# Layer 1 of a hybrid encoder: which engine combines probability chunks, and how the sub-norm's sums of squares are multiplied

## The chip, the cores and the metric

The kernel runs on one core of a Trainium2 chip. The metric is the device time of one execution in microseconds (us). The engines of a core run their own instruction queues in order and wait for each other by semaphores: PE is TensorE (matmuls; PEld is its weight load), DVE is VectorE, ACT is ScalarE, POOL is GpSimd, SP issues most DMAs.

## What is computed

A two-layer encoder trunk over 2048 tokens of width 1024, in float32. Layer 0 (a sliding-window attention and a chunked attention, side by side) is not touched here. Layer 1 is a differential attention with 8 heads; cut to what matters:

```python
s1 = einsum(q1, k1) * scale          # 8 heads, q and k of width 64
s2 = einsum(q2, k2) * scale
p1 = softmax(where(mask, s1, -1e30))
p2 = softmax(where(mask, s2, -1e30))
a = p1 - lam * p2
o = einsum(a, v)                     # v of width 128 per head
...
o = rms_norm(o, subln_g) * (1.0 - lambda_init)   # per head, over the 128 values
y = (o.reshape(b, s, C_W) * silu(gate)) @ w_out
return x + y
```

The mask lets a block of 64 queries see all earlier blocks of 64 keys and its own.

## The kernel before

The kernel runs layer 0, then layer 1's input projection, then layer 1's mixer, `_mix1`. All that is told here lies in `_mix1`.

Tokens are cut into `NB` = 4 blocks (b) of 512, each with 4 rows of 128 queries (j). The work goes head by head and block by block, 32 pairs (h, b), here called heads for short: first the pairs with b = 0 and 1 in turn for each h (16 of them), then the 8 with b = 2, then the 8 with b = 3. For a pair, `scores` computes for each row and for both maps m (the two softmaxes) the scores of its keys in chunks of up to 512. For one chunk, PE makes two matmuls into a PSUM bank named cS (L913, L914, with queries split in a high and a low part), DVE finds the negative maximum cnm of each row (L917), and ACT writes the exponential into a probability tile named cP (L920). The bank of cS is free once ACT has read it; there are 4 of them.

After both maps of a row are done, DVE works out the reciprocals of the sums (crl, L931, L932), and each pair of chunks (one of each map) is joined to one: p1 is scaled by its reciprocal on POOL (L936), and then p2 is scaled and added. That second step has two forms. Ordinarily POOL scales p2 (L945) and adds it (L946). For every `COMB`-th pair, counted over the whole layer in `count`, DVE does both in one instruction (L943), for which it first multiplies two small factors (L942, tile cc) where a row has more than one chunk:

```python
nc.gpsimd.tensor_scalar(p1, p1, rl[:, 0:1], e1, ALU.mult, ALU.mult)
count[0] += 1
if count[0] % self.COMB == 0:
    ...
    nc.vector.scalar_tensor_tensor(p1, p2, c2, p1, ALU.mult, ALU.add)
else:
    nc.gpsimd.tensor_scalar(p2, p2, rl[:, 1:2], e2, ALU.mult, ALU.mult)
    nc.gpsimd.tensor_tensor(p1, p1, p2, ALU.add)
```

There are 320 such pairs of chunks in the layer.

`values` then transposes the joined chunks on PE (ctr, L959), copies each transposed tile out of PSUM into a tile cpt on ACT or, every third time, on DVE (L962, L964), and multiplies it with v into the output cO (L966, in float32, which stands as two records for each matmul in the trace). At the end of a head, `gate` copies cO out on ACT (cot, L981), squares it (csq, L983), makes part of the gate's sigmoid (L985, L986) and multiplies by the gate on POOL (L987). The rest of the head's sub-norm, `rest`, is put off to the third key tile of the next head's `values` (for the last head it follows at once): one float32 matmul with a tile of ones sums the squares over the 128 values (cms, L991, again two records), ACT takes the logarithm (L992), DVE adds (L993), ACT takes the exponential (L994), DVE multiplies (L995), and the result is split into high and low parts for the output projection.

Beside this main stream runs a side stream of PE work paced by a table (`STAGES1`): first the gate's projection (cG), then the output projection (com), both as three matmuls of rounded products (float32 rounded to the multiplier's format, dtype fp32r) at L214 to L216 per term. Values trail the scores by `LAG1` units. The order on each engine's queue is set when the program is built, by a scheduler that estimates each instruction's length and puts next what it takes to be ready; so a change of one instruction can shift the order of others nearby.

The pools: p1's chunks live in the pool `pp` with 20 buffers, p2's in 8 buffers of `sb`, the copied transposes in 6 buffers (tag "pt") of `sb`. A chunk's buffer of `pp` is held from its exponential to the last transpose that reads it.

Of the kernel before, what the change touches and what calls it, by code (L numbers as in the profile page):

```python
# [10 lines left out]
F32 = mybir.dt.float32  # L11
F32R = mybir.dt.float32r
AF = mybir.ActivationFunctionType
ALU = mybir.AluOpType
# [4 lines left out]
P = 128  # L19
# [4 lines left out]
BLK = NTB * P  # L24
# [7 lines left out]
def f32(ap):  # L32
    return ap.bitcast(F32)
# [52 lines left out]
class Trunk:  # L86
# [1 line left out]
    AHEAD = 2  # L88
    BANKS0, LAG0, SHARE0 = (3, 3, 1, 1), 9, 0.85
    FIN = 18  # L90
    COMB = 5
    BANKS1, LAG1 = (4, 2, 1, 1), (30, 30, 36, 36)
    STAGES1 = ((0, 0), (44, 84), (1088, 504))

# [762 lines left out]
    def _mix1(self, es):  # L857
        nc, tc, a, s = self.nc, self.tc, self.a, self.s1
        n = "c"
        pool = lambda nm, bufs, **kw: es.enter_context(tc.tile_pool(name=n + nm, bufs=bufs, **kw))  # L860
# [2 lines left out]
        ld = pool("ld", 2)  # L863
        yp = pool("y", 2 * KT)
        vp = pool("v", 4)
        pp = pool("pp", 20)
        kp = pool("kp", 4)
        sb = pool("sb", 2)
        NS, NTR, NO, NM = self.BANKS1
# [4 lines left out]
        mm = nc.tensor.matmul  # L874
# [17 lines left out]
        def scores(h, b, q, K, res, then):  # L892
# [4 lines left out]
            for j in range(NTB):  # L897
# [35 lines left out]
                for z, (c, ce) in enumerate(cuts):  # L933
# [3 lines left out]
                    count[0] += 1  # L937
                    if count[0] % self.COMB == 0:
                        c2 = rl[:, 1:2]
# [9 lines left out]
        def values(h, b, res):  # L949
            us = res["u"]  # L950
            O = pO.tile([P, BLK], F32, tag="O", name=n + "O")
            nkt = (b + 1) * NTB
            for kt in range(nkt):
                j0 = max(0, kt - b * NTB)
                wd = (NTB - j0) * P
                tp = ptr.tile([P, 512], F32, tag="tr", name=n + "tr")
                kk = (kt % 4) * P
                for j in range(j0, NTB):
                    nc.tensor.transpose(tp[:, (j - j0) * P:(j - j0 + 1) * P], us[j][kt // 4][:, kk:kk + P], self.ident)  # L959
                T = sb.tile([P, 512], F32, tag="pt", name=n + "pt", bufs=6)  # L960
                if kt % 3:
                    nc.scalar.activation(T[:, :wd], tp[:, :wd], AF.Copy)  # L962
                else:
                    nc.vector.tensor_copy(T[:, :wd], tp[:, :wd])  # L964
                v = res["v"][kt // 4][:, kk:kk + P]
                mm(O[:, j0 * P:], v, T[:, :wd], start=(kt == 0), stop=(kt == nkt - 1), skip_group_check=True)  # L966
                if kt == 2:
                    while normal:
                        normal.pop(0)()
                yield wd / P  # L970
            gate(h, b, O)
# [3 lines left out]
        def gate(h, b, O):  # L975

            rows, tok = slice(h * P, (h + 1) * P), slice(b * BLK, (b + 1) * BLK)
            g = sb.tile([P, BLK], F32, tag="g", name=n + "gg")
            nc.sync.dma_start(g, s["g"][rows, tok])
            o = ot.tile([P, BLK], F32, tag="ot", name=n + "ot")  # L980
            nc.scalar.activation(o, O, AF.Copy)  # L981
            sq = sb.tile([P, BLK], F32, tag="sq", name=n + "sq", bufs=1)
            nc.scalar.activation(sq, o, AF.Square)  # L983
            sg = sb.tile([P, BLK], F32, tag="sg", name=n + "sg", bufs=1)
            nc.scalar.activation(sg, g, AF.Exp, scale=-1.0)  # L985
            nc.scalar.activation(sg, sg, AF.Ln, bias=self.one)  # L986
            nc.gpsimd.tensor_tensor(o, o, g, ALU.mult)  # L987

            def rest():
                ms = ptr.tile([P, BLK], F32, tag="tr", name=n + "ms")  # L990
                mm(ms, f32(self.ones), sq, start=True, stop=True)  # L991
                nc.scalar.activation(sq, ms, AF.Ln, bias=self.eps, scale=1.0 / P)  # L992
                nc.vector.scalar_tensor_tensor(sg, sq, 0.5, sg, ALU.mult, ALU.add)  # L993
                nc.scalar.activation(sg, sg, AF.Exp, scale=-1.0)  # L994
                nc.vector.scalar_tensor_tensor(o, o, self.sub, sg, ALU.mult, ALU.mult)  # L995
                if b == 0 or (h, b) in place:
                    split(h, b, o)
                else:
                    nc.sync.dma_start(s["o"][rows, tok], o)
                ended.add((h, b))  # L1000

            normal.append(rest)
# [7 lines left out]
        def split(h, b, o):  # L1010
            yH, yL = y_tiles(h, b)
            nc.scalar.activation(yH, o, AF.Copy)
            nc.gpsimd.tensor_tensor(yL, o, f32(yH), ALU.subtract)
            y[b][h] = yH, yL
# [123 lines left out]
        def heads():  # L1138
# [7 lines left out]
            for (h, b), nxt in zip(order, order[1:] + [None]):  # L1146
                at[0] = b
                after, spare = [None, {}], NB - keys(b)
                new = nxt and nxt[0] != h
                if nxt and not new:  # L1150
                    after[1] = K

                def then(j, m, z):
                    if (j, m, z) == (2, 0, 0) and nxt:
                        after[0] = load_q(*nxt)
                    if (j, z) == (1, 0) and new:
                        for i in range(min(spare, keys(nxt[1]))):
                            after[1][i, m] = load_k(nxt[0], i, m)
                    if j == NTB - 1:
                        if new and z + spare < keys(nxt[1]):  # L1160
                            after[1][z + spare, m] = load_k(nxt[0], z + spare, m)
                        if m == 0 and z not in V:
                            V[z] = load_v(h, z)

                res = {}
                yield from scores(h, b, q, K, res, then)
                res["v"] = [V[z] for z in range(b + 1)]
                if new:
                    V = {}
                queue.append(values(h, b, res))  # L1170
                q, K = after
# [64 lines left out]
```

## Time and profile before

| what | value |
|---|---|
| median of 3 runs | 2839.93 us (2833.36 to 2840.09) |
| profiled execution | 2843.39 us, of which the span from the first to the last instruction is 2841.6 us |
| mean granted TensorE clock | 0.987 |
| busy over the span | PE 2707.3 us (95%), DVE 1844.8 (65%), ACT 1543.8 (54%), POOL 1596.6 (56%) |
| the chain that ended last | PE 73%, DVE 9%, DMA 9%, ACT 4% of the span |
| layer 1's mixer | from about 1810 us to the end |

A group's row in the profile reads: line, engine, operation, tiles written and read, form, count, then busy us and mean ns of one, then the engine's idle time ahead of these instructions and who ended it. A row of the timeline reads: start in us, length in us, engine, line, operation, tiles, form, count. A row of waits reads: who waited for whom, total us, times, the longest. A row of windows gives for each stretch of the span the busy us of each engine with its instruction count, the granted clock and the DMA load.

### The profile page before, as it was taken

Reading aid. Unit: us, or ns where it says so; the run is one execution under the profiler, and the core shown is the slowest. Engines: PE = TensorE matmul, PEld = TensorE weight load, DVE = VectorE, ACT = ScalarE, POOL = GpSimd, SP = SyncE. Lnnn points to the kernel's source line nnn. Section 1 sums busy time; section 2 is a strip of 40 time slices with the busy share of each in tenths; the row PEclk is TensorE's granted clock in tenths of the full one; section 3 lists DMA queues with packets and bytes.
Section 4 is the critical chain, followed back from the end, with each engine's and each line's share of the span. In section 5 each row is a group of like instructions: output and inputs, shape, how many; then the busy total and the mean of one; then the engine's idle time right before and its main releaser. Section 6 shows DMA issues by size and latency. Waiting matters only on the chain.

```text
span 2841.6 us, 43911 instructions
## 1 busy us (share of the span) xinstructions
PE 2707.3 (95%) x13384; PEld 2171.4 (76%) x13384; DVE 1844.8 (65%) x4643; ACT 1543.8 (54%) x4015; POOL 1596.6 (56%) x1740
## 2 busy tenths in 40 slices
PE   7999999999899999899999999899999999999998
PEld 5888888887788888777788888777676777676766
DVE  7752285347788886498808870468787777666651
ACT  4443543367766666243334331468787676666751
POOL 3541252234545454267745560468888887888871
PEclk9999999999999999999999999999999999999999
DMA  5674343738887765476885443887868676464542
GB/s 161 228 233 149 108 140 120 220 117 232 218 197 186 190 181 150 155 271 198 254 255 189 141 126 108 251 251 212 248 187 232 180 212 207 120 191 131 176 137 81
DMA packets 356092, 521.68 MB, mean 184 GB/s; under 512 B 44816, under 2 KB 139792, under 8 KB 355856
## 3 DMA queue, kind: packets, MB, share of 16 engines
q1 hardware_dynamic: 355856, 518.87, 61.6%
q8 instruction: 107, 1.75, 0.3%
q14 instruction: 129, 1.06, 0.1%
HBM read 361.70 MB, written 157.02 MB: 183 GB/s over the span
## 4 chain that ended last, share of the span: by engine, by line
PE 73%; DVE 9%; DMA 9%; ACT 4%; issue 2%; POOL 2%; SPq 1%; DVEq 0%; ACTq 0%; POOLq 0%
PE cO L966 7%; PE p1mm L214 5%; PE p1mm L216 5%; PE p1mm L215 5%; PE cS L913 4%; PE cS L914 4%; PE ctr L959 3%; PE p0mm L214 3%; PE p0mm L216 3%; PE p0mm L215 3%; PE com L214 2%; PE com L215 2%; PE com L216 2%; PE mom L214 2%; PE cG L214 2%
## 5 line engine op out<-in xcount | busy, mean ns | idle before, releaser
L920 ACT ACTIVATE cP<-cS,cnm 128x512 f32<-128x512 f32 (+3 forms) x640 | 397.3, 628 | 181.6 <-DVE cnm L917 142.9
L917 DVE TENSOR_REDUCE cnm<-cS 128x1 f32<-128x512 f32 (+3 forms) x640 | 371.7, 601 | 80.0 <-PE cS L914 74.1
L936 POOL TENSOR_SCALAR cP<-cP,crl,ce 128x512 f32<-128x512 f32 (+3 forms) x288 | 220.0, 778 | 164.2 <-DVE crl L931 84.7
L215 PE MATMUL p1mm<-p1wL,p1hH 128*128 128x512 f32 x768 | 302.3, 394 | 0.4 <-POOL p1wL L310 0.4
L214 PE MATMUL p1mm<-p1wH,p1hH 128*128 128x512 f32 x768 | 301.1, 393 | 0.8 <-ACT p1wH L308 0.8
L216 PE MATMUL p1mm<-p1wH,p1hL 128*128 128x512 f32 x768 | 301.8, 393 | 0.0
L310 POOL TENSOR_TENSOR p0wL<-p0ws,p0wH 128x512 fp32r<-128x512 f32 (+1 forms) x124 | 149.4, 1237 | 266.8 <-ACT p0wH L308 257.8
L966 PE MATMUL cO<-cpt,cv 128*128 128x512 f32 (+3 forms) x640 | 287.7, 537 | 4.2 <-DVE cpt L964 3.6
L946 POOL TENSOR_TENSOR cP<-cP,cP 128x512 f32<-128x512 f32 (+3 forms) x256 | 285.5, 1140 | 1.4
L913 PE MATMUL cS<-ck,cqd 128*128 128x512 f32 (+3 forms) x640 | 261.2, 413 | 12.4 <-ACT cP L920 7.1
L214 PE MATMUL p0mm<-p0wH,p0hH 128*128 128x512 f32 (+1 forms) x640 | 239.9, 377 | 5.2 <-ACT p0vt L472 3.5
L310 POOL TENSOR_TENSOR p1wL<-p1ws,p1wH 128x512 fp32r<-128x512 f32 x128 | 169.2, 1342 | 133.6 <-ACT p1wH L308 126.4
L216 PE MATMUL p0mm<-p0wH,p0hL 128*128 128x512 f32 (+1 forms) x640 | 239.6, 375 | 1.8 <-DVE p0hL L336 1.8
L215 PE MATMUL p0mm<-p0wL,p0hH 128*128 128x512 f32 (+1 forms) x640 | 239.2, 374 | 0.0
L914 PE MATMUL cS<-ck,cql 128*128 128x512 f32 (+3 forms) x640 | 231.4, 367 | 4.4 <-DMA cql<-qL 4.4
L959 PEld LDWEIGHTS ctr<-ident,cP 128*128 128x128 f32 x1088 | 136.8, 141 | 109.7 <-issue 60.8
L945 POOL TENSOR_SCALAR cP<-cP,crl,ce 128x512 f32<-128x512 f32 (+3 forms) x230 | 180.0, 795 | 0.0
L959 PE MATMUL ctr<-ident,cP 128*128 128x128 f32 x1088 | 172.9, 274 | 0.8 <-ACT cpt L962 0.3
L214 PEld LDWEIGHTS p1mm<-p1wH,p1hH 128*128 128x128 f32 x768 | 144.7, 188 | 29.8 <-ACT p1wH L308 1.0
L215 PEld LDWEIGHTS p1mm<-p1wL,p1hH 128*128 128x128 f32 x768 | 144.7, 188 | 29.5 <-POOL p1wL L310 0.8
L216 PEld LDWEIGHTS p1mm<-p1wH,p1hL 128*128 128x128 f32 x768 | 144.7, 188 | 28.8
L913 PEld LDWEIGHTS cS<-ck,cqd 128*128 128x128 f32 x640 | 121.9, 191 | 44.6 <-ACT cP L920 19.9
(306 smaller groups left out, 7271.1 us busy)
## 6 DMA issues: line engine op xcount, KB each, us to landing
p1ws<-in_od_w_in_dram SPq DMA_DIRECT2D x56, 512.0 KB, 4.4
p0ws<-in_ev_w_in_dram SPq DMA_DIRECT2D x48, 512.0 KB, 4.4
ck<-kH SPq DMA_DIRECT2D x144, 128.0 KB, 3.3
ck<-kL SPq DMA_DIRECT2D x144, 128.0 KB, 3.5
cv<-v SPq DMA_DIRECT2D x72, 256.0 KB, 4.5
cqd<-qH SPq DMA_DIRECT2D x128, 128.0 KB, 4.6
cql<-qL SPq DMA_DIRECT2D x128, 128.0 KB, 4.6
cwH<-wgH SPq DMA_DIRECT2D x64, 256.0 KB, 4.6
```

The lines of the kernel that those rows point to most:

```text
L214: mm(ps, aH, bH, start=first, stop=False)
L215: mm(ps, aH, bL, start=False, stop=False)
L216: mm(ps, aL, bH, start=False, stop=last)
L310: low.tensor_tensor(l[:, :width], ws[:, k, :width], f32(h[:, :width]), ALU.subtract)
L913: mm(ps, qd[:, m, js], kt[:, :wd], start=True, stop=False)
L914: self.anchor = mm(ps, ql[:, m, js], kt[:, :wd], start=False, stop=True).ins
L917: nc.vector.tensor_reduce(nm[:, m, z:z + 1], ps, AX.X, ALU.max, negate=True)
L920: nc.scalar.activation(chunks[z][:, :wd], ps, AF.Exp, bias=nm[:, m, z:z + 1], accum_out=acc)
L936: nc.gpsimd.tensor_scalar(p1, p1, rl[:, 0:1], e1, ALU.mult, ALU.mult)
L946: nc.gpsimd.tensor_tensor(p1, p1, p2, ALU.add)
L959: nc.tensor.transpose(tp[:, (j - j0) * P:(j - j0 + 1) * P], us[j][kt // 4][:, kk:kk + P], self.ident)
L966: mm(O[:, j0 * P:], v, T[:, :wd], start=(kt == 0), stop=(kt == nkt - 1), skip_group_check=True)
```

## The change

Three things, all in layer 1's mixer.

1. `COMB` goes from 5 to 3: DVE joins every third pair of chunks, POOL the other two.
2. The sub-norm's sum of squares is made of two rounded products: right after the square, ACT writes a rounded copy csH, DVE subtracts it from the square and writes the rounded rest csL, and in `rest` two matmuls with dtype fp32r take the place of the float32 one. The sum is the same up to rounding.
3. The two new tiles of 128 x 512 take the place of one buffer of `pp` (19 for 20) and one of the copied transposes (5 for 6).

```diff
-    COMB = 5
+    COMB = 3
...
-        pp = pool("pp", 20)
+        pp = pool("pp", 19)
...
-                T = sb.tile([P, 512], F32, tag="pt", name=n + "pt", bufs=6)
+                T = sb.tile([P, 512], F32, tag="pt", name=n + "pt", bufs=5)
...
             nc.scalar.activation(sq, o, AF.Square)
+            sH = sb.tile([P, BLK], F32R, tag="sH", name=n + "sH", bufs=1)
+            sL = sb.tile([P, BLK], F32R, tag="sL", name=n + "sL", bufs=1)
+            nc.scalar.activation(sH, sq, AF.Copy)
+            nc.vector.tensor_tensor(sL, sq, f32(sH), ALU.subtract)
...
                 ms = ptr.tile([P, BLK], F32, tag="tr", name=n + "ms")
-                mm(ms, f32(self.ones), sq, start=True, stop=True)
+                mm(ms, self.ones, sH, start=True, stop=False)
+                mm(ms, self.ones, sL, start=False, stop=True)
```

Counted over the program's instructions, DVE's joins (L943) go from 64 to 106 and its small factors (L942) from 58 to 98; POOL loses 42 scalings and 42 additions; ACT gains 32 copies, DVE 32 subtractions; PE has 32 float32 matmuls of 512 columns fewer and 64 rounded ones more. Layer 0 and layer 1's projection keep their instructions and their order.

How the order moves is shown at two places. The first is PE's queue around the sub-norm matmul of the second head, which stands among the first key tiles of the next head. Before:

```order
L966 MATMUL cO<-cpt,cv 128x384
L966 MATMUL cO<-cpt,cv 128x256
L991 MATMUL cms<-csq,ones 128x512
L959 MATMUL ctr<-ident,cP_21508 128x128
L913 MATMUL cS<-ck_21687,cqd 128x384
```

The same place in the changed program (the numbers in names of tiles are those of the program and differ between the two):

```order
L966 MATMUL cO<-cpt,cv 128x384
L966 MATMUL cO<-cpt,cv 128x256
L913 MATMUL cS<-ck_21693,cqd 128x384
L914 MATMUL cS<-ck_21693,cql 128x384
L995 MATMUL cms<-csH,ones 128x512
L959 MATMUL ctr<-ident,cP_21512 128x128
L913 MATMUL cS<-ck_21752,cqd 128x384
L914 MATMUL cS<-ck_21752,cql 128x384
L996 MATMUL cms<-csL,ones 128x512
```

The first rounded product has moved behind one pair of score matmuls, and the second behind a transpose and another pair.

The second place is DVE's queue in the 29th head (b = 3), ahead of the sub-norm's addition csg. Before:

```order
L932 TENSOR_SCALAR crl<-crl,nlam 128x1
L942 TENSOR_SCALAR cc_32307<-ce,crl 128x1
L943 SCALAR_TENSOR_TENSOR cP_32226<-cP_32265,cc_32307,cP_32226 128x512
L917 TENSOR_REDUCE cnm<-cS 128x1
L916 MEMSET cS 64x64
L993 SCALAR_TENSOR_TENSOR csg<-csq,csg 128x512
```

The same place in the changed program, some rows further ahead of csg:

```order
L917 TENSOR_REDUCE cnm<-cS 128x1
L987 TENSOR_TENSOR csL<-csq,csH 128x512
L917 TENSOR_REDUCE cnm<-cS 128x1
L942 TENSOR_SCALAR cc_32293<-ce,crl 128x1
L942 TENSOR_SCALAR cc_32303<-ce,crl 128x1
L943 SCALAR_TENSOR_TENSOR cP_32196<-cP_32247,cc_32293,cP_32196 128x512
L917 TENSOR_REDUCE cnm<-cS 128x1
L943 SCALAR_TENSOR_TENSOR cP_32233<-cP_32278,cc_32303,cP_32233 128x512
L917 TENSOR_REDUCE cnm<-cS 128x1
```

Where one join stood, a row of four chunks now often has two, and the subtraction csL stands among the maxima cnm just ahead of them.

## The prediction

> **What bounds the kernel now.** I read the page's chain of work first, then the table of windows over layer 1's mixer, then PE's waits there. The chain that ended last is PE's:
>
> ```profile
> PE 73%; DVE 9%; DMA 9%; ACT 4%; issue 2%; POOL 2%; SPq 1%; DVEq 0%; ACTq 0%; POOLq 0%
> ```
>
> Only the mixer changes, so its stretches count: the heads with b = 0 and 1, those with b = 2, those with b = 3, and the tail.
>
> ```profile
> core 0: us, PE busy (x) PEld busy (x) DVE busy (x) ACT busy (x) POOL busy (x), PEclk, DMA share, GB/s
> 1810.00:2115.00 305.00, 293.36 (x1368) 219.82 (x1368) 221.93 (x652) 221.84 (x643) 235.47 (x281) 0.99 0.81 231
> 2115.00:2405.00 290.00, 286.32 (x1314) 209.65 (x1313) 221.32 (x511) 206.62 (x588) 234.94 (x265) 1.00 0.71 207
> 2405.00:2806.00 401.00, 388.01 (x1715) 277.44 (x1713) 245.99 (x554) 243.63 (x655) 310.07 (x334) 0.98 0.49 146
> 2806.00:2841.60 35.60, 27.56 (x110) 21.44 (x110) 6.66 (x10) 2.51 (x4) 2.54 (x2) 0.95 0.28 96
> ```
>
> PE is busy 96 to 99% of the first three; POOL 77 to 81%, DVE 61 to 76%, ACT 61 to 73%. A busy PE can still be held inside its records, so I look at what its idle time waits for, over the whole mixer (1810 us to the end):
>
> ```profile
> PE cS L913 <- ACT cP L920: 7.1, 11, 1.3
> PE com L214 <- ACT cyk L1012: 3.7, 1, 3.7
> PE com L214 <- DVE cxr L1088: 3.6, 2, 2.5
> PE cO L966 <- DVE cpt L964: 3.6, 4, 2.1
> PE cms L991 <- ACT csq L983: 1.3, 1, 1.3
> PE cO L966 <- ACT cpt L962: 0.4, 1, 0.4
> PE ctr L959 <- POOL cP L946: 0.3, 1, 0.3
> ```
>
> Three things are to be seen. PE almost never waits for POOL (0.3 us), so relieving POOL has no direct price. The largest wait, 7.1 us, is for a score bank that ACT has yet to read. And all the waits for engines are some 20 us of 1031.6: work taken off PE is time, unless a new wait takes its place.
>
> **The sub-norm's matmul, PE's term.** Today's, between its neighbours, in PE's timeline in the early heads:
>
> ```profile
> 2050.68 1.02 PE L991 MATMUL cms<-csq,ones 128*128 128x512 f32 x2
> 2051.54 0.27 PE L959 MATMUL ctr<-ident,cP 128*128 128x128 f32 x1
> ...
> 2052.00 0.39 PE L214 MATMUL cG<-p1hH,cwH 128*128 128x512 f32 x1
> 2052.23 0.40 PE L215 MATMUL cG<-p1hL,cwH 128*128 128x512 f32 x1
> 2052.46 0.40 PE L216 MATMUL cG<-p1hH,cwL 128*128 128x512 f32 x1
> 2052.70 0.33 PE L913 MATMUL cS<-ck,cqd 128*128 128x384 f32 x1
> ```
>
> Records overlap, so I count from start to start. The two passes of the float32 matmul hold PE from 2050.68 to 2051.54, 0.86 us. A rounded matmul of the same 512 columns holds it 0.23 us (2052.00 to 2052.23 to 2052.46). Two of them cost 0.46, so each head saves 0.40 us.
>
> ```profile
> L991 PE MATMUL cms<-csq,ones 128*128 128x512 f32 x64 | 33.6, 607 | 1.3 <-ACT csq L983 1.3
> ```
>
> The 64 records are 32 heads. The last head's matmul lies in the exposed tail and is counted there; the other 31 give 31 x 0.40 = **12.4 us less**.
>
> **The tail.** After the last cO nothing covers the chain of the last sub-norm:
>
> ```profile
> 2805.93 0.63 ACT L983 ACTIVATE csq<-cot 128x512 f32<-128x512 f32 x1
> ...
> 2806.61 1.12 PE L991 MATMUL cms<-csq,ones 128*128 128x512 f32 x2 [1.35 <-ACT csq L983]
> ...
> 2807.78 0.69 ACT L992 ACTIVATE csq<-cms,eps 128x512 f32<-128x512 f32 x1 [1.22 <-PE cms L991]
> 2808.50 0.69 DVE L993 SCALAR_TENSOR_TENSOR csg<-csq,csg 128x512 f32<-128x512 f32 x1 [3.77 <-ACT csq L992]
> 2809.22 0.63 ACT L994 ACTIVATE csg<-csg 128x512 f32<-128x512 f32 x1 [0.76 <-DVE csg L993]
> 2809.94 0.75 DVE L995 SCALAR_TENSOR_TENSOR cot<-cot,sub,csg 128x512 f32<-128x512 f32 x1 [0.75 <-ACT csg L994]
> ```
>
> From the matmul's start to ACT's next step are 1.17 us. In its place come a rounded copy, a subtraction and the second product (the first runs beside the subtraction). The copy is taken at 0.65 with its hand-over (ACT's steps here take 0.63), the subtraction at 0.72 (DVE's step at 2808.50 to the next start), and the last product at half of 1.17, 0.58: 1.95 us. That is **0.8 us more**.
>
> **What it adds to DVE and ACT, and takes from POOL.** The nearest groups:
>
> ```profile
> L943 DVE SCALAR_TENSOR_TENSOR cP<-cP,cc,cP 128x512 f32<-128x512 f32 (+3 forms) x58 | 54.9, 946 | 19.4 <-POOL cP L936 18.8 <-DMA cwH<-wgH 0.5
> L942 DVE TENSOR_SCALAR cc<-ce,crl 128x1 f32<-128x1 f32 x57 | 11.7, 205 | 1.1
> L993 DVE SCALAR_TENSOR_TENSOR csg<-csq,csg 128x512 f32<-128x512 f32 x32 | 27.7, 866 | 19.3 <-ACT csq L992 19.1 <-ACT csg L986 0.2
> L995 DVE SCALAR_TENSOR_TENSOR cot<-cot,sub,csg 128x512 f32<-128x512 f32 x32 | 33.3, 1040 | 5.3 <-ACT csg L994 3.0 <-POOL cP L945 2.0
> L1012 ACT ACTIVATE cy<-coy 128x512 fp32r<-128x512 f32 x19 | 12.1, 638 | 16.5 <-DMA coy<-o 16.5
> L945 POOL TENSOR_SCALAR cP<-cP,crl,ce 128x512 f32<-128x512 f32 (+3 forms) x230 | 180.0, 795 | 0.0
> L946 POOL TENSOR_TENSOR cP<-cP,cP 128x512 f32<-128x512 f32 (+3 forms) x256 | 285.5, 1140 | 1.4
> ```
>
> and three waits of the mixer:
>
> ```profile
> DVE cP L943 <- POOL cP L936: 21.1, 24, 2.0
> ACT cP L920 <- POOL cP L945: 12.4, 8, 2.5
> ACT cP L920 <- PE ctr L959: 6.1, 11, 1.7
> ```
>
> POOL loses 42 x (0.795 + 1.140) = 81 us, none of it on the path. DVE gains 42 joins at 0.946 (39.7 us), 40 small factors at 0.205 (8.2) and 32 subtractions, which no row shows: bounded by csg (0.866) and cot (1.040), taken at 0.95 (30.4). That is 78 us of work. A join also stands in DVE's queue until POOL has scaled p1, 21.1 us over 64 joins, 0.33 each; 42 more add 14 us. So DVE is held for about 92 us more, of 336 us in which it is idle (1031.6 less the 695.9 of the windows' sum). ACT gains 32 x 0.64 = 20 us and stays under 70%.
>
> Behind a waiting join or subtraction stand the maxima cnm; for these the exponentials wait, and for the bank that an exponential frees the next score matmul: that is the 7.1 us above. Here both ends are known only roughly. PE's waits for exponentials and copies are 7.1 + 3.6 + 0.4 = 11.1 us. If they come from all of DVE's 696 us alike, 92 more cost 92 x 11.1 / 696 = 1.5 us. If today's 64 joins alone cause them (64 x (0.95 + 0.20 + 0.33) = 95 us), 92 more cost 10.8 us. Below nothing: with POOL's 81 us gone, p2's buffers come free sooner and ACT's 12.4 us of waiting for them shrinks; PE sees at most the 7.1 us of its own wait for banks. I take **1.5 us more**: joins are a small part of DVE's work, and 11 waits stand against 64 joins.
>
> **The buffers.** With 20 of them, exponentials already wait 6.1 us for a transpose to free one, in 11 cases; with 19, the program has 61 exponentials whose wait names PE, in place of 43. In a queue where PE has other work meanwhile I take nothing for PE, with 6 us more (the 6.1 doubled) as the upper end. The copies of transposes go from 6 to 5, while only two PSUM banks feed them; nothing. The matmul for the squares has to wait for two steps more, and the order of the changed program has put it behind further PE work: in the second head, in the rows shown above, two pairs of score matmuls and a transpose. This covers the subtraction, at no cost; if the cover fails, it is up to 1.6 us a head.
>
> **The sum.** -12.4 + 0.8 + 1.5 = -10.1 us. The profiled execution took 2843.39 us (span 2841.6 and 1.8 around it), so 2833.3 for one like it. It lies 3.5 us above the median of the runs, 2839.93; carried over as a difference, the forecast is **2829.8 us**. 0.3%, about what a measurement of this kernel can tell from no change, is 8.5 us: the border of faster is at 2831.4, and of slower at 2848.4.
>
> **Rivals.**
>
> *The gain is eaten by waits behind the joins.* The upper end above: 10.8 us for 1.5, so -12.4 + 0.8 + 10.8 = -0.8, 2839.1 us. For it speaks that PE's largest wait is in just that place; against it, that DVE is idle a third of the mixer.
>
> *POOL's relief reaches PE.* Up to 7.1 us more gained, with nothing lost: -12.4 + 0.8 - 7.1 = -18.7, 2821.2 us. For it speaks that POOL is the busiest engine beside PE and that ACT waits 12.4 us for it; against it, PE's own 0.3 us.
>
> *DVE becomes the bound where its new work comes together.* In the 29th head's rows of the changed program the subtraction and two joins stand among four maxima. Such a cluster holds the queue 0.95 + 2 x (0.95 + 0.33) = 3.5 us. Four score banks cover 4 x 0.46 = 1.8 us of score matmuls if PE has nothing else, so PE would stand 1.7 us. Half of the 42 added joins, 21, may make such clusters: 21 x 1.7 = 36 us, net +24, 2864 us. It decides against the change from 20.1 / 21 = 0.96 us a cluster on (11.6 for the gain and 8.5 for the border). For it: in the early heads DVE would be held 222 + 15 x 1.48 + 16 x 0.95 = 259 of 305 us (15 of the 42 joins and 16 subtractions are there), 85%. Against it: PE's longest wait for a bank is 1.3 us, and score matmuls stand between transposes, cO and the side stream, which lengthen the cover.
>
> By the Trainium skill, page "SBUF — State Buffer", section "Who interferes with whom", a VectorE instruction with two SBUF inputs and a GpSimd instruction that reads SBUF exclude each other, and the later one waits for the whole of the other. The trace agrees in direction: csg took 0.69 us at 2808.50 with POOL idle and 0.866 in the mean, cot 0.75 at 2809.94 and 1.040 in the mean. By that rule the 74 added instructions could each stand behind a whole POOL addition of 1.14 us, 84 us of DVE, where the excess in the rows (about 0.3) gives 22; it would bring the last rival's 2864 nearer.
>
> **How the numbers follow.** The forecast's case, 2825 to 2836, has 0.58, of which 0.40 lies below 2831.4. POOL's relief has 0.10, the eaten gain 0.20, DVE as the bound 0.12. So faster 0.50, same 0.38 (0.18 and 0.20), slower 0.12. The range goes from 2821, the relief's time, to 2847: the eaten gain's 2839.1 with the 6 us of the buffers and measurement; it leaves out the slower case and little else.
>
> **What would show it.** Right: the sub-norm's two products take 0.46 us from start to start, PE's count of waits for cP and cpt stays near 11 us, and the mixer is some 10 us shorter. The tail step is right if ACT's logarithm starts 1.9 to 2.0 us after the last square has ended. Wrong: waits of cS on cP, or of cms on csL, of 10 us or more; cnm's idle time going over from PE to DVE's own joins; or exponentials that wait for transposes far beyond 6 us.

## The result, and the profile after

The changed kernel is slower. Its median is 2854.18 us (6 runs, 2850.51 to 2859.25) beside 2839.11 (6 runs, 2833.36 to 2840.8) of the kernel before: the ratio is 1.0051 with a 95% interval of 1.0036 to 1.0066, some 15 us. The forecast was 2829.8, so even the sign was wrong. The profiled execution took 2855.26 us, with a span of 2853.5 us against 2841.6, and a granted clock of 0.982 against 0.987.

The changed kernel's chain of work that ended last, shares by engine:

```profile
PE 69%; DVE 9%; DMA 7%; ACT 4%; POOL 2%; issue 2%; SPq 1%; DVEq 0%; ACTq 0%; POOLq 0%
```

Its windows over the same stretches as before (columns: stretch, length, busy us of each engine with its instructions, granted clock, DMA):

```profile
core 0: us, PE busy (x) PEld busy (x) DVE busy (x) ACT busy (x) POOL busy (x), PEclk, DMA share, GB/s
1810.00:2115.00 305.00, 289.69 (x1371) 220.03 (x1369) 241.86 (x697) 229.64 (x661) 223.11 (x255) 0.99 0.79 230
2115.00:2405.00 290.00, 280.28 (x1278) 207.14 (x1277) 224.05 (x534) 202.50 (x577) 218.04 (x233) 0.98 0.67 201
2405.00:2806.00 401.00, 379.89 (x1687) 275.74 (x1686) 263.64 (x590) 246.33 (x662) 287.76 (x304) 0.97 0.48 147
```

For the whole mixer the window has to start at the mixer's first score matmul, so that all of its 4608 matmul records are in it: 1780.4 us before, 1775.2 in the changed kernel. (From 1810 us on, 106 of them would be cut off before and 128 here.) The row of before, then that of the changed kernel:

```profile
1780.40:2841.60 1061.20, 1019.59 (x4608) 748.61 (x4608) 710.56 (x1778) 687.09 (x1928) 793.72 (x896) 0.99 0.64 188
```

```profile
1775.20:2853.50 1078.30, 1017.24 (x4608) 754.04 (x4608) 756.43 (x1892) 701.63 (x1960) 745.26 (x812) 0.97 0.62 185
```

PE has less to do and still ends later. It is busy 1017.2 us, where it was 1019.6: only 2.4 less. And it is idle 1078.3 - 1017.2 = 61.1 us, where it was 1061.2 - 1019.6 = 41.6: 19.5 more. So the mixer has grown by 17.1 us; the span grew by 11.9, since in this execution the mixer also began 5.2 us earlier. What PE waited for in the mixer (who on whom, total us, times, longest):

```profile
PE cS L913 <- ACT cP L920: 19.5, 20, 5.1
...
PE cO L966 <- DVE cpt L964: 3.4, 4, 1.2
PE cO L966 <- ACT cpt L962: 2.2, 4, 1.2
PE cms L995 <- ACT csH L986: 2.1, 1, 2.1
PE cms L996 <- DVE csL L987: 1.9, 3, 0.9
```

The wait for a score bank has gone from 7.1 us in 11 cases to 19.5 in 20, and the longest from 1.3 to 5.1. That is 12.4 us of the 19.5; the waits for cpt and for the sub-norm's halves are a few us more. The longest one can be followed back over three engines. PE's timeline there:

```profile
2721.07 0.73 PE L214 MATMUL com<-p1hH,cy 128*128 128x512 f32 x1 [2.18 <-DVE cxr L1093]
2721.59 0.63 PE L215 MATMUL com<-p1hL,cy 128*128 128x512 f32 x1
2722.02 0.63 PE L216 MATMUL com<-p1hH,cy 128*128 128x512 f32 x1
2727.79 0.80 PE L913 MATMUL cS<-ck,cqd 128*128 128x512 f32 x1 [5.14 <-ACT cP L920]
```

PE stands 5.14 us for ACT's exponential, and ACT has been waiting for the maximum cnm:

```profile
2726.96 0.69 ACT L920 ACTIVATE cP<-cS,cnm 128x512 f32<-128x512 f32 x1 [10.56 <-DVE cnm L917]
```

DVE's queue, and what POOL did meanwhile:

```profile
2720.93 5.39 DVE L943 SCALAR_TENSOR_TENSOR cP<-cP,cc,cP 128x512 f32<-128x512 f32 x1
2726.25 1.27 DVE L917 TENSOR_REDUCE cnm<-cS 128x1 f32<-128x512 f32 x2
```

```profile
2720.84 1.27 POOL L991 TENSOR_TENSOR cot<-cot,cgg 128x512 f32<-128x512 f32 x1
2722.07 3.70 POOL L946 TENSOR_TENSOR cP<-cP,cP 128x512 f32<-128x512 f32 x3
```

One join took 5.39 us: from just after POOL began the gate's multiplication until 0.55 us after the last of three additions (2725.77). By the profile it wasn't waiting for a semaphore (no idle time stands ahead of the record); its execution itself was that long. Two maxima stood behind it. PE's next wait in length for a score bank, 3.54 us from 2203.70 on, likewise stands behind one long DVE instruction, here over four additions:

```profile
2198.55 5.71 DVE L998 SCALAR_TENSOR_TENSOR csg<-csq,csg 128x512 f32<-128x512 f32 x1 [0.46 <-ACT csq L997]
```

```profile
2198.70 5.01 POOL L946 TENSOR_TENSOR cP<-cP,cP 128x512 f32<-128x512 f32 x4
```

Around such gaps PE also gets half its clock for a while: the matmuls at 2721.59 and 2722.02, between a wait of 2.18 us and the one of 5.14, start 0.43 us apart, where 0.23 is usual. Two windows show it, one ahead of that stretch and one over it:

```profile
2710.00:2721.00 11.00, 8.89 (x45) 7.11 (x43) 5.33 (x15) 4.77 (x13) 9.65 (x12) 1.00 0.88 253
2721.20:2731.40 10.20, 5.06 (x13) 3.57 (x14) 8.07 (x8) 2.90 (x8) 4.58 (x4) 0.50 0.51 164
```

### The profile page after: what moved, and what is told of

Same layout as the page of the kernel before. It is cut to its first block, busy times and chain, and to the rows that moved or that the text cites. A ratio compares the mean times of both kernels' runs of the same rounds, so it can differ in the third digit from the quotient of the medians.

```text
span 2853.5 us, 43958 instructions
## 1 busy us (share of the span) xinstructions
PE 2707.3 (95%) x13384; PEld 2177.7 (76%) x13384; DVE 1886.9 (66%) x4757; ACT 1558.6 (55%) x4047; POOL 1548.6 (54%) x1656
## 4 chain that ended last, share of the span: by engine, by line
PE 69%; DVE 9%; DMA 7%; ACT 4%; POOL 2%; issue 2%; SPq 1%; DVEq 0%; ACTq 0%; POOLq 0%
PE cO L966 7%; PE p1mm L216 5%; PE p1mm L214 5%; PE p1mm L215 5%; PE cS L913 3%; PE cS L914 3%; PE ctr L959 3%; PE p0mm L216 2%; PE p0mm L214 2%; PE p0mm L215 2%; PE com L214 2%; PE mom L214 2%; PE com L215 2%; PE com L216 2%; PE mom L215 2%
## 5 line engine op out<-in xcount | busy, mean ns | idle before, releaser
L936 POOL TENSOR_SCALAR cP<-cP,crl,ce 128x512 f32<-128x512 f32 (+3 forms) x288 | 222.5, 787 | 216.1 <-DVE crl L931 121.0
L913 PE MATMUL cS<-ck,cqd 128*128 128x512 f32 (+3 forms) x640 | 261.9, 413 | 24.3 <-ACT cP L920 19.5
L946 POOL TENSOR_TENSOR cP<-cP,cP 128x512 f32<-128x512 f32 (+1 forms) x214 | 250.6, 1191 | 1.9
L913 PEld LDWEIGHTS cS<-ck,cqd 128*128 128x128 f32 x640 | 122.9, 192 | 57.1 <-ACT cP L920 31.8
L945 POOL TENSOR_SCALAR cP<-cP,crl,ce 128x512 f32<-128x512 f32 (+3 forms) x190 | 159.5, 851 | 0.0
```

The source lines that it names most:

```text
L913: mm(ps, qd[:, m, js], kt[:, :wd], start=True, stop=False)
```

## The experiments

All kernels are compared with the kernel before, run on the same chip within the same batch (its medians there are 2838.92, 2840.72, 2840.25 and 2838.92 us). The theories on trial, as they came up: that one of the three **parts** does it (the joins, the split of the squares, the buffers); that the **order** does it, which the scheduler makes anew after any edit; and that a **lock** does it, in which DVE instructions with two inputs in SBUF are held up by POOL's runs of additions.

### One part at a time

Kernel before, with `COMB` alone changed:

```diff
-    COMB = 5
+    COMB = 3
```

> The joins alone: every third pair on VectorE, float32 matmul for the squares and the buffers (20 and 6) as before. Theory J (the added joins cost: they read two tiles of SBUF, stand behind GpSimd's runs of additions, and make the maxima and so PE's score banks late): slower than before by 10 to 25 us, with PE waits of cS on cP well above 7 us. Theory B (the smaller buffers cost): within 5 us of before. Theory O (only the changed order, by luck): anything within 15 us.

Measured: 2842.51 us, ratio 1.0015 (1.0000 to 1.0029). In this one order the 42 joins alone cost next to nothing.

The changed kernel, with `COMB` set back, so the split and the smaller pools alone:

```diff
-    COMB = 3
+    COMB = 5
```

> The changed kernel with every fifth pair on VectorE as before: the two rounded products and the smaller buffers alone. Theory J: the PE term of 12.4 us is kept, less the tail's 0.8 to 2 us: 8 to 12 us faster than before. Theory B: slower than before by 0 to 15 us, since the buffers stay small. Theory S (the added copy and subtraction stand in the way of the exponentials): about as slow as the changed kernel, 10 to 15 us over before.

Measured: 2861.35 us, 1.0074 (1.0052 to 1.0095): slower than the whole change, with PE's 12.4 us of relief in it and none of the added joins. So in these two orders the joins aren't what costs.

Kernel before, with the smaller pools alone:

```diff
-        pp = pool("pp", 20)
+        pp = pool("pp", 19)
...
-                T = sb.tile([P, 512], F32, tag="pt", name=n + "pt", bufs=6)
+                T = sb.tile([P, 512], F32, tag="pt", name=n + "pt", bufs=5)
```

> The kernel before with 19 and 5 buffers in place of 20 and 6, nothing else. Theory J: within 4 us of before. Theory B: 10 to 25 us slower, with exponentials waiting for transposes (6.1 us before) two to four times as long, and PE idle for cP with them.

Measured: 2858.95 us, 1.0070 (1.0049 to 1.0091), 20 us more. If it were the buffers as such, exponentials would wait for the transposes that free them. Two of its waits:

```profile
PE cS L913 <- ACT cP L920: 21.4, 24, 3.5
...
ACT cP L920 <- PE ctr L959: 7.5, 11, 1.4
```

They hardly do: 7.5 us for 6.1 before, and no copy of a transpose waits for the product that frees its buffer. But the wait for a score bank is 21.4 us, as in the changed kernel.

Kernel before, where only the counter that says which pairs DVE joins starts elsewhere. The amount of work is the same, every fifth pair, but other ones:

```diff
-        count = [0]
+        count = [2]
```

> The kernel before with its counter of pairs started at 2 in place of 0: as many joins on VectorE (64), on other pairs. It prices the luck of the order. Theory J: within 5 us of before. Theory O: 5 to 15 us away from before, as far as the changed kernel is.

Measured: 2863.19 us, 1.0081 (1.0058 to 1.0104). An edit that adds, removes and shrinks nothing costs 24 us, more than the whole change. That leaves the order as the candidate, and it means that none of the results above is the price of a part.

### How far the order spreads both kernels

Other starts of the same counter, for the kernel before (1 and 3) and for the changed one (1 and 2):

```diff
-        count = [0]
+        count = [1]
```

> The kernel before with its counter started at 1 in place of 0 (2 gave 24 us more). Theory O: again 5 to 25 us over before, since before's order is a favourable one among many. If 2 was an unlucky one and before is typical: within 6 us of before.

> The changed kernel with its counter of pairs started at 1: as many joins, on other pairs, another order. Theory O: somewhere from 2825 to 2870 us, with no relation to the changed kernel's 2854. If the change itself costs 15 us: 2850 to 2860 us.

```diff
-        count = [0]
+        count = [3]
```

> A fourth order of the kernel before (counter from 3). If before's own order is a favourable one: 2850 to 2875. If two bad ones were drawn by chance: 2835 to 2845.

```diff
-        count = [0]
+        count = [2]
```

> A third order of the changed kernel (counter from 2). If the loss is the order's: between 2835 and 2870, and the mean of the changed kernel's orders not above that of the orders of before (2839, 2863, 2869). If the change costs: at or above 2850.

Measured, with the ratio to the kernel before and its interval, and the earlier rows beside them:

| counter starts at | before | changed |
|---|---|---|
| 0 | 2839.11 | 2854.18, 1.0051 (1.0036 to 1.0066) |
| 1 | 2869.15, 1.0096 (1.0078 to 1.0113) | 2847.70, 1.0029 (1.0015 to 1.0043) |
| 2 | 2863.19, 1.0081 (1.0058 to 1.0104) | 2844.59, 1.0020 (1.0009 to 1.0031) |
| 3 | 2840.82, 1.0012 (0.9998 to 1.0026) | |

The kernel before spreads over 30 us, and the one that the change started from is, with the start at 3, the best of its four. The changed kernel's three lie between 2845 and 2854, and the tested one is its worst. The means are 2853.1 and 2848.8, and so few orders with such a spread don't tell them apart. With the start at 1 or 2 the same change would have been measured as faster by about 20 us.

The wait for a score bank doesn't tell a good order from a bad one. The slowest order of the kernel before (start at 1) has less of it than the fastest (7.1 us):

```profile
PE cG L214 <- DMA cwH<-wgH: 13.5, 3, 6.1
...
PE cS L913 <- ACT cP L920: 5.8, 12, 2.3
```

With the start at 2 it is 11.0 us, at 3 it is 9.0. What the slowest order does have, from the mixer's start on and with the same work, is 14.3 us more idle time on PE (56.0 for 41.6) and 12.1 us more busy time (1031.7 for 1019.6). Its clock stood at half for 66.4 us of the mixer, where it was 30.4; PE was busy in 50.8 and 24.4 us of that. At half the clock that is some 13 us of busy time more, an estimate that covers the 12.1.

### What in the order costs: a bench of the join beside POOL

A bench of its own, without the trunk: eight DVE instructions in a row, of one kind at a time, beside eight POOL instructions in a row. The core of it:

```diff
+    for i in range(8):
+        gt(y, y, e, ALU.subtract)
+    for i in range(8):
+        stt(x, x, 0.5, c, ALU.mult, ALU.add)
```

> Not the trunk: a few instructions alone, in stages, the output filled with a tile of them. VectorE runs eight joins of 128x512 (two SBUF inputs) by themselves, beside eight GpSimd additions, beside eight GpSimd scalings, and beside four groups of scale, scale, add; then eight with one input in PSUM, eight maxima (one input) and eight 128x8 products beside additions. Theory L: alone about 0.6 us a join; beside the run of additions the first join stands still until the run's end, 8 to 10 us, or most of it; beside scalings, with one input in PSUM, and for maxima no such stand. Rival (VectorE and GpSimd take turns, each waits for one instruction of the other): no join above 2.0 us in any stage.

DVE's groups (the join's form alone at L62, beside additions at L69, beside scalings at L74, with one input from PSUM beside additions at L86, maxima beside additions at L91):

```profile
L69 DVE SCALAR_TENSOR_TENSOR x<-x,c 128x512 f32<-128x512 f32 x8 | 12.1, 1515 | 0.2
...
L74 DVE SCALAR_TENSOR_TENSOR x<-x,b 128x512 f32<-128x512 f32 x8 | 7.6, 944 | 0.2
L62 DVE SCALAR_TENSOR_TENSOR x<-x,b 128x512 f32<-128x512 f32 x8 | 5.5, 691 | 5.0 <-DMA b<-in_x_dram 4.9
L86 DVE SCALAR_TENSOR_TENSOR x<-q,x 128x512 f32<-128x512 f32 x8 | 5.5, 691 | 0.2
L91 DVE TENSOR_REDUCE r<-x 128x1 f32<-128x512 f32 x8 | 5.5, 686 | 0.2
```

With two inputs in SBUF the mean goes from 0.691 to 1.515 us beside additions, and to 0.944 beside scalings. With one input in PSUM, and for maxima, it stays at 0.69. That is the exclusion, with its prices. But it isn't 5 us: in the bench the two engines take turns.

A second bench gives POOL additions that don't depend on each other, as they are in the trunk, with a small product or two joins beside them:

```diff
+    for i in range(8):
+        gt(z[i], y, z[i], ALU.subtract)
+    stt(x, x, sx[:, 0:1], b, ALU.mult, ALU.add)
+    stt(x, x, 0.5, c, ALU.mult, ALU.add)
```

> Instructions alone again, now with GpSimd's eight additions independent of each other, as in the trunk. Theory L: a VectorE instruction with two SBUF inputs that meets the run ends only with the run: one of the four 128x8 products, and one of the two joins beside the second run, take 5 to 11 us. Rival (turns, as with additions that depend on each other): none above 2 us. Beside eight independent scalings the four joins take under 1.2 us each in both.

DVE's timeline, then POOL's:

```profile
9.05 4.78 DVE L61 TENSOR_TENSOR sx<-sx,sy 128x8 f32<-128x8 f32 x4
...
24.99 1.65 DVE L68 SCALAR_TENSOR_TENSOR x<-x,sx,b 128x512 f32<-128x512 f32 x1
26.67 1.63 DVE L69 SCALAR_TENSOR_TENSOR x<-x,c 128x512 f32<-128x512 f32 x1
```

```profile
24.83 10.69 POOL L67 TENSOR_TENSOR z<-y,z 128x512 f32<-128x512 f32 x8
```

Again turns: 1.65 and 1.63 us a join, and 4.78 / 4 = 1.2 us for a product of 128 x 8, which takes 0.16 us alone. The theory that a DVE instruction is held for a whole run of additions isn't borne out by either bench, though the trunk's trace shows just that at 2720.93. What differs in the trunk (a DVE queue with other instructions, the transfers, the operands' places) wasn't settled.

### An order written out: POOL's additions never in a row

In both kernels POOL's queue has up to four scalings, then up to four scalings, then up to four additions in a row. This edit binds it to scale, scale, add, pair by pair: a pair's scalings may be issued only after the addition of the pair ahead. For the kernel before:

```diff
+        added = [None]
...
-                    nc.gpsimd.tensor_scalar(p1, p1, rl[:, 0:1], e1, ALU.mult, ALU.mult)
+                    with tc.issue_after(added[0]) if added[0] is not None else nullcontext():
+                        nc.gpsimd.tensor_scalar(p1, p1, rl[:, 0:1], e1, ALU.mult, ALU.mult)
...
-                        nc.gpsimd.tensor_scalar(p2, p2, rl[:, 1:2], e2, ALU.mult, ALU.mult)
-                        nc.gpsimd.tensor_tensor(p1, p1, p2, ALU.add)
+                        with tc.issue_after(added[0]) if added[0] is not None else nullcontext():
+                            nc.gpsimd.tensor_scalar(p2, p2, rl[:, 1:2], e2, ALU.mult, ALU.mult)
+                        added[0] = nc.gpsimd.tensor_tensor(p1, p1, p2, ALU.add).ins
```

> The kernel before, with GpSimd's queue bound so that each pair's two scalings and its addition stand together (scale, scale, add, scale, scale, add), where before all scalings of a row come first and then three or four additions in a row. Same work on each engine. Theory L (a VectorE instruction with two SBUF inputs stands still for a whole run of GpSimd's additions, and this is what makes score banks late): VectorE's tiny product cpe, up to 4.15 us long before, stays under 1.5 us, the time that joins, csg, cot and cpe take together falls by 30 us or more, PE's idle time falls, and the kernel is 5 to 20 us faster than before. Theory O (luck of the order only): no fixed sign, 0 to 25 us slower like the shifted counter.

The same edit in the changed kernel:

> The changed kernel with the same binding of GpSimd's queue. Theory L: the 5.4 us join and the 5.7 us addition csg of the changed kernel become under 2 us, PE's waits for cP fall from 19.5 us to under 10, and the kernel is 15 to 30 us faster than the changed one, so 5 to 15 us faster than before, the 12.4 us of the rounded products coming through. Theory O: within 15 us of the changed kernel, either side.

Then, with that edit in place, the other variants: the kernel before with the counter started at 1, the kernel before with `COMB` at 3, the changed one with `COMB` at 5, and the changed one with the counter started at 1.

> GpSimd's queue bound as in the faster version of before, and the counter started at 1, which without the binding cost 30 us (2869). Theory L (the luck of the order is in the main how many of GpSimd's runs meet a VectorE instruction with two SBUF inputs): within 8 us of the bound kernel's 2827, so below 2835. Theory O (luck has other sources): 2845 to 2860.

> GpSimd's queue bound and every third pair on VectorE, float32 matmul and buffers (20 and 6) as before. If the 42 added joins are what eats the PE term in the bound changed kernel (2832): 2835 to 2845 us. If they cost nothing once GpSimd's additions come singly: 2822 to 2832.

> GpSimd's queue bound, the two rounded products and the smaller buffers, every fifth pair on VectorE. If with the binding the PE term comes through where VectorE has few joins: 2813 to 2820 us, 7 to 14 under the bound kernel before. If the copy and the subtraction (two more SBUF inputs for VectorE) or the buffers eat it: 2825 to 2835.

> The bound changed kernel with its counter started at 1. If the change is worth its PE term once the runs are broken: 2815 to 2825, below both orders of the bound kernel before (2826.9 and 2832.5). If it is worth nothing: 2826 to 2838.

Measured medians, free and bound, with the ratio of the bound kernel to the kernel before. PE's idle time in the profiled execution is the length of the mixer's window (from its first score matmul, at 1772 to 1783 us, to the end) less PE's busy time in it, free and bound:

| kernel | free | bound | ratio | idle, free | idle, bound |
|---|---|---|---|---|---|
| before | 2839.11 | 2826.90 | 0.9957 (0.9942 to 0.9972) | 41.6 | 39.8 |
| before, count 1 | 2869.15 | 2832.54 | 0.9968 (0.9954 to 0.9983) | 56.0 | 36.8 |
| before, COMB 3 | 2842.51 | 2829.51 | 0.9962 (0.9949 to 0.9975) | 46.5 | 36.3 |
| changed, COMB 5 | 2861.35 | 2826.87 | 0.9953 (0.9936 to 0.9971) | 57.1 | 42.5 |
| changed | 2854.18 | 2832.16 | 0.9970 (0.9954 to 0.9987) | 61.1 | 46.8 |
| changed, count 1 | 2847.70 | 2827.31 | 0.9960 (0.9945 to 0.9974) | 55.4 | 41.0 |

The rows that the last column comes from, for the first and the fifth kernel (windows over the mixer, of the bound kernel before and of the bound changed one):

```profile
1777.50:2830.70 1053.20, 1013.37 (x4608) 749.94 (x4608) 676.02 (x1778) 687.27 (x1928) 797.29 (x896) 0.98 0.64 189
```

```profile
1774.60:2830.60 1056.00, 1009.24 (x4608) 750.52 (x4608) 724.19 (x1892) 702.83 (x1960) 746.58 (x812) 0.98 0.64 189
```

All six are faster bound than free, by 12 to 37 us, and what spread over 30 us lies within 6. The bound versions beat both kernels; the best measured are the bound kernel before and the bound changed one with `COMB` at 5, about 13 us under the kernel before. The change itself is worth nothing that can be told: bound, with the counter at 0 and 1, the kernel before takes 2826.9 and 2832.5, the changed one 2832.2 and 2827.3, a mean of 2829.7 for both.

PE's wait for a score bank, first in the bound kernel before (7.1 us free), then in the bound changed one (19.5 free):

```profile
PE cS L914 <- ACT cP L921: 8.2, 10, 2.3
```

```profile
PE cS L914 <- ACT cP L921: 8.5, 15, 1.9
```

In the changed kernel the binding thus does most of what theory L expected: the wait falls under 10 us and the time by 22, but the 12.4 us of the rounded products don't come through. In the kernel before it does so only in part: PE's idle time, which was to fall, falls by 1.8 us, and its busy time by 6.2 with the same work. What shortened its records wasn't settled.

How DVE's instructions meet POOL's additions has changed with it. DVE's groups of the kernel before, free, bound, and free with the counter at 1 (the second number behind the bar is the mean ns of one):

```profile
L929 DVE TENSOR_TENSOR cpe<-ce,cla 128x4 f32<-128x4 f32 (+2 forms) x96 | 54.5, 567 | 48.4 <-ACT ce L928 47.8
```

```profile
L945 DVE SCALAR_TENSOR_TENSOR cP<-cP,cc,cP 128x512 f32<-128x512 f32 (+3 forms) x58 | 46.6, 803 | 21.5 <-POOL cP L938 20.3 <-DMA cqd<-qH 0.5
L930 DVE TENSOR_TENSOR cpe<-ce,cla 128x4 f32<-128x4 f32 (+2 forms) x96 | 34.9, 363 | 34.5 <-ACT ce L929 34.2
```

```profile
L929 DVE TENSOR_TENSOR cpe<-ce,cla 128x4 f32<-128x4 f32 (+2 forms) x96 | 63.8, 665 | 38.5 <-ACT ce L928 37.8
L943 DVE SCALAR_TENSOR_TENSOR cP<-cP,cc,cP 128x512 f32<-128x512 f32 (+3 forms) x58 | 58.3, 1006 | 21.3 <-POOL cP L936 20.6
```

The product cpe, at most 8 columns wide, takes 0.567 us in the mean in the kernel before, 0.665 in its slower order and 0.363 bound; the join 0.946, 1.006 and 0.803. Summed over all DVE instructions in the mixer with two inputs in SBUF (the joins, cpe, csL, csg and cot), that is 176 us before, 192 with the counter at 1, and 143 bound; for the changed kernel 230, and 199 bound; the longest is 1.73 and 1.85 us in the two bound kernels, 4.15 and 5.71 in the free ones. Of these instructions, those longer than 2 us, so longer than any join in the benches, number 7 in the kernel before, 14 with the counter at 1, and none in either order bound; the changed kernel has 3, and bound none. So the meetings differ with the order, and the binding ends the long ones. That they are what it gains by isn't shown, since it changes the rest of the order too. And they aren't all that the order decides: the kernel before with the counter at 2 has a sum of 178, like the one at 0, and takes 24 us more (its profiled execution, the shortest of its six, 11 us more). What makes that difference stays open.

## Why the prediction was wrong

**The sub-norm's matmul, right.** In PE's timeline of the changed kernel in the early heads, the first product to the next start:

```profile
2057.94 0.39 PE L995 MATMUL cms<-csH,ones 128*128 128x512 f32 x1
2058.17 0.28 PE L913 MATMUL cS<-ck,cqd 128*128 128x256 f32 x1
...
2058.40 0.40 PE L996 MATMUL cms<-csL,ones 128*128 128x512 f32 x1
2058.72 0.50 PE L913 MATMUL cS<-ck,cqd 128*128 128x512 f32 x1
```

It is 0.23 us for the first and 0.32 for the second; over the mixer both mostly take 0.23 to 0.24, and 0.31 to 0.63 right behind a transpose or a float32 matmul, whose last pass then lies in their record. So the 0.46 a head was right, and PE should have lost about 12 us of busy time. It fell only by 2.4. The sum has no term for the clock: it stood at half for 58.0 us of the mixer, where it was 30.4 before, and PE was busy in 40.0 and 24.4 us of that. At half the clock that is, as an estimate, (40.0 - 24.4) / 2 = 7.8 us more of busy time. The other 2 us stay open.

**The tail, too small.** The last head's chain now:

```profile
2815.94 0.63 ACT L983 ACTIVATE csq<-cot 128x512 f32<-128x512 f32 x1
2816.60 0.63 ACT L986 ACTIVATE csH<-csq 128x512 fp32r<-128x512 f32 x1
2816.70 1.27 POOL L991 TENSOR_TENSOR cot<-cot,cgg 128x512 f32<-128x512 f32 x1 [19.14 <-ACT csq L983]
2817.26 1.26 DVE L987 TENSOR_TENSOR csL<-csq,csH 128x512 fp32r<-128x512 f32 x1 [2.58 <-ACT csH L986]
...
2819.11 0.69 ACT L997 ACTIVATE csq<-cms,eps 128x512 f32<-128x512 f32 x1 [1.88 <-PE cms L996]
```

From the end of the square (2816.57) to the logarithm are 2.54 us, where 1.9 to 2.0 were expected and 1.22 stood before (2806.56 to 2807.78): 1.3 more, not 0.8. The subtraction took 1.26 us for my 0.72, while POOL's gate multiplication ran until 2817.97; csL has two inputs in SBUF. The Trainium skill, page "SBUF — State Buffer", section "Who interferes with whom", would have said so: whoever of the two engines issues first keeps the other out for the whole instruction. This row agrees: csL began 0.71 us ahead of the end of POOL's instruction and ended 0.55 us behind it.

**The waits behind joins and subtractions: here the forecast failed.** The step is the one that ends in "I take **1.5 us more**: joins are a small part of DVE's work, and 11 waits stand against 64 joins". PE's idle time rose by 19.5 us in its place, 12.4 of it in exactly the wait that the step named; that is above the upper end of 10.8 too. (The waits for engines that the prediction put at some 20 us in all are 24.6, with three rows that it doesn't show: 3.1 for cy, 1.2 for cgt, 0.3 for cpt.) The work that went into the step was forecast well:

```profile
L943 DVE SCALAR_TENSOR_TENSOR cP<-cP,cc,cP 128x512 f32<-128x512 f32 (+2 forms) x98 | 96.4, 984 | 29.4 <-POOL cP L936 28.9
```

With eight more at 6.2 us the joins take 102.6 us, 41.8 more; the subtractions take 31.3 and the small factors 7.3 more, in all 80 us for the forecast's 78. DVE's wait for POOL's scaling rose from 21.1 to 34.9 us, 13.8 for 14. (cpe took 18.0 us less, and records overlap, so that DVE's busy time rose by 45.9.) What failed is the price in PE's time of a us for which DVE is held. No such price shows: with the 42 joins alone the wait for a bank was 8.8 us and the kernel took 2842.5, while without any added instruction the wait went from 5.8 us (counter at 1) to 21.4 (smaller pools). What the step took from the trace of before, the 7.1 us of waits for banks and the longest of 1.3, wasn't a property of the work. It belongs to one order, and that one of the two good ones of four. The orders with the counter at 1 and 2 have the same work and cost 30 and 24 us more. The change made the scheduler plan anew, so the base on which the forecast stood was gone. This was not among the rivals. That it is the order, and not the added work, which makes the 15 us is borne out by the bound kernels, where before and changed, two orders each, have the same mean: there the added work takes back the gain, and no more. Which places in the order make the 15 us is traced for the two longest waits alone.

**The buffers.** "I take nothing for PE, with 6 us more (the 6.1 doubled) as the upper end". Exponentials do wait longer for a transpose, as two of the changed kernel's waits show:

```profile
ACT cP L920 <- PE ctr L959: 15.2, 13, 3.9
...
ACT cP L920 <- POOL cP L945: 5.3, 7, 1.4
```

That is 15.2 us for 6.1. With the smaller pools alone it is 7.5, while the time is 20 us more; so the 20 us come by another way than the one priced. Whether fewer buffers cost anything in an equal order wasn't tried.

**POOL's relief.** ACT's wait for POOL's scaling went from 12.4 to 5.3 us, as the rival said, and PE saw nothing of it.

**DVE as the bound where its work clusters.** This rival had the right sign and the right place: the long waits for a bank stand behind DVE. It priced the number of joins, though, and the kernel with the joins alone speaks against that, free (2842.5) and bound (2829.5, between the two bound orders of before). What stood in the queue at 2720.93 was one join of 5.39 us, not a cluster of 3.5. The sentence on the skill's rule pointed there and had too small a weight.

**What the runs leave open.** Bound, the change saves PE 4.1 us of busy time (1013.4 to 1009.2), and 5.4 with the counter at 1 (1013.1 to 1007.6), and PE is idle 6.9 and 4.1 us more, which takes it back. The traces don't show which of the added instructions does that, and a difference of a few us is within the spread of single orders.

## What to carry to other kernels

Where a scheduler sets the order, a trace shows one draw of it: before a change of half a per cent is priced from the waits of that trace, or judged by one measurement, make two or three neutral edits (here, another start of a counter) to see how far equal work spreads, and compare the change over several of them. If the spread is larger than the gain, bind the order that matters first: a few lines on POOL's queue were worth more (12 to 37 us) than the change. Of DVE's instructions with two inputs in SBUF count not only how many there are but what POOL runs beside them, and where the order is yours, try to keep POOL's two-input instructions from standing in a row.

## What the hardware showed

- A VectorE instruction with two inputs in SBUF that takes 0.691 us alone took 1.63 beside GpSimd's additions and 0.944 in the mean beside its scalings; a product of 128 x 8 went from 0.16 to 1.2 us. With one input in PSUM it took 0.691, and a maximum 0.686, beside the same additions. A TENSOR_SCALAR with one 128x512 input and a factor for each row took 1.33 to 1.51 beside them; its time alone wasn't measured. Both engines pay: eight additions took 13.31 us beside eight joins and 10.66 beside eight with one input in PSUM.
- In the trunk one such instruction took 5.39 us, until 0.55 us after one multiplication and three additions of GpSimd's, and another 5.71, over four additions. No join in the benches took more than 1.65, so this is seen and not explained.
- Around PE's waits of 2 to 5 us (once 1.15) the granted clock goes to 0.50, in the changed kernel's mixer in eight stretches of 3.41, 6.83 or 10.24 us, so multiples of 3.41 us (one is the window 2721.2 to 2731.4 above). The Trainium skill, page "TensorE: Matmul & The Clock Gate", section "What's actually happening", gives 3413 ns for the window by which the clock is set, and the trace agrees. Such a wait thus costs more than its own length, by what PE does at half speed behind it.
